# A hybrid-attention encoder layer: the last 448 tokens' attention moved beside the first 640 tokens' feed-forward

## The chip, the cores and the metric

The kernel runs on one core of a Trainium2 chip. The core has a matrix engine (PE, TensorE), two elementwise engines that are used for most of the rest (DVE, VectorE, and POOL, GpSimd), an engine for functions and copies (ACT, ScalarE), and a queue (SP, SyncE) from which this kernel issues its DMA transfers. The metric is device time of one execution in microseconds (us).

## The reference

One layer over 1024 prompt tokens and 64 sample tokens with a past of 128 keys, d_model 1024, in float32. Eight heads use stick-breaking attention (sb: no softmax, a product of keep-probabilities along the keys), eight use forgetting attention (fox: softmax with a cumulative bias).

```python
h = rmsnorm(x, g_mix) * (1.0 + scale) + shift
parts = jnp.split(h @ w_in, SPLITS, axis=-1)          # q, k, v of sb and of fox, forget gates
...
log_keep = jnp.where(mask, jax.nn.log_sigmoid(-z), 0.0)              # sb, z = q k / 8
between = lax.cumsum(log_keep, axis=3, reverse=True) - log_keep
a = jnp.where(mask, jnp.exp(jax.nn.log_sigmoid(z) + between), 0.0)
...
p = jax.nn.softmax(jnp.where(mask, s, -jnp.inf), axis=-1)            # fox, s = q k / 8 + fq - fk
...
o = jnp.concatenate([rmsnorm(o_sb.reshape(b, t, SB_WIDTH), g_sb_out),
                     rmsnorm(o_fx.reshape(b, t, FOX_WIDTH), g_fox_out)], axis=-1)
x = x + (1.0 + ada[2]) * (o @ w_o)
h = rmsnorm(x, g_ffn) * (1.0 + ada[4]) + ada[3]
f = (jax.nn.silu(h @ w_gate) * (h @ w_up)) @ w_down                  # 2816 hidden columns
return x + (1.0 + ada[5]) * f
```

A final rmsnorm follows; k, v and the log forget gates are outputs too.

## The kernel before

The activations stand transposed, features on the partitions and tokens along the columns, in three chunks CH of 384, 384 and 320 tokens. Every dense product splits both sides into a high and a low part (fp32r) and takes three matmuls for each block of 128 rows (dense, L422): high times high, low weight times high, high weight times low. A weight tile (512 KB) is loaded as wraw, copied to its high part on ACT and subtracted to its low part on DVE or POOL (split, L171).

For each of eight pairs of heads (sb for pairs 0 to 3, fox for 4 to 7) the kernel runs attention on the pair (L667) and then project_pair, values and setup for the next one (L472, L529, L561) and some of the 16 ada jobs (L766), which compute the six modulation vectors. Attention takes a head's nine query tiles of 128 tokens in the order QT. A tile computes scores into the PSUM bank ps_z (qs against k2 and kl, the high and low parts of k), then the weights a_t: for sb two sigmoids on ACT, a scan over kp on DVE (L711) and a product on POOL (L715); for fox a maximum on DVE, exp on ACT and a product with the reciprocal sum l on POOL (L738). The weights are turned block by block on PE (pt_a, L747), split into the two halves of aT on ACT and DVE (L753), multiplied with the values vv into ps_av (L756) and written to oT_d in DRAM (av_out). The profile shows a block's transpose as one row of pt_a, so a tile with w keys has w/128 of them.

During the attention of the last pairs the sb outputs are read back from oT_d, squared and summed (o_stats, L820), read again, normed and split (sb_norm L859, sb_split); during the last pair the fox outputs follow (fox_prep). Then come the output projection (out_block, acc_o, evacuated into x1 with the residual at L1014 and L1022), the second norm (norm2, L1061) and the FFN for all tokens: eleven groups of two tiles of 128 hidden columns, each with gate and up products (banks gu), silu, the hidden tile split into dh and dl, and the down product of the group (acc_d, L1217 to L1219), which DVE adds to x1 (L1222):

```python
            for c in range(3):
                t0, n = CH[c]
                for m in range(KT):
                    acc = bank(("t", "t", "acc")[m % 3], "acc_d")
                    for i in range(G):
```

The order of instructions on each engine isn't the order of the code: the program is built in a context that moves instructions by a timeline of its own, within what buffers and banks allow. PSUM has eight banks, given out by tags: acc 1, z 3, t 2, u 1, av 1.

## Time and profile before

| | before |
|---|---|
| median of 3 runs (lowest to highest) | 1682.59 us (1679.03 to 1685.3) |
| profiled execution | 1681.39 us, span 1679.2 us |
| mean granted clock of PE | 0.978 |
| busy over the span | PE 1580.3 us (94%), DVE 947.0, ACT 657.1, POOL 604.9 |
| DMA | 141.61 MB, mean 84 GB/s |

Busy time counts an instruction from start to end; matmuls are pipelined, so one that stands alone is counted with its latency, longer than the distance at which matmuls follow each other in an unbroken row. The program has about 9,700 matmuls. Attention and everything ahead of the FFN end at about 870 us; the FFN fills 870 to 1640.

### The profile page before, as it was taken

The page shows a single profiled execution, that of the slowest core. Times are in us where ns is not written, and L with a number is a line of the kernel's source. Part 1 is how long each engine was busy: PE and PEld are TensorE (multiplying, and loading weights), DVE is VectorE, ACT ScalarE, POOL GpSimd, SP SyncE. Part 2 cuts the span into 40 slices and gives each one's busy share as a digit, 9 for nine tenths or more (in the row PEclk, how much of TensorE's full clock was granted, in tenths as well). Part 3 has the DMA queues.
Part 4 walks back from the last instruction along what each step waited for, and adds up shares of the span by engine and source line. Part 5 has one row for each costly group of instructions (what it writes and reads, how often), then busy time and mean ns, then how long its engine had stood idle before and what let it go on. Part 6 is the DMA issues. An engine that isn't in the chain of part 4 may idle for free.

```text
span 1679.2 us, 26182 instructions
## 1 busy us (share of the span) xinstructions
PE 1580.3 (94%) x9822; PEld 1487.7 (89%) x9822; DVE 947.0 (56%) x1828; ACT 657.1 (39%) x1410; POOL 604.9 (36%) x556
## 2 busy tenths in 40 slices
PE   8898998988899977998999999999999999999998
PEld 4697887867888966987989999999999999999997
DVE  5659767598557565676895334334443344334336
ACT  5466656577445553555454021120211112021127
...
GB/s 309 165 102 93 110 92 100 93 78 32 125 121 121 151 144 63 114 184 100 91 101 63 2 76 39 38 51 26 76 15 62 51 26 71 6 76 50 27 26 107
DMA packets 174750, 141.61 MB, mean 84 GB/s; under 512 B 14336, under 2 KB 167584, under 8 KB 174624
## 3 DMA queue, kind: packets, MB, share of 16 engines
...
## 4 chain that ended last, share of the span: by engine, by line
PE 65%; DVE 4%; POOL 2%; DMA 1%; ACT 1%; issue 1%; SPq 1%; DVEq 0%; POOLq 0%; ACTq 0%
PE gu L428 10%; PE gu L429 10%; PE gu L427 10%; PE acc_d L1219 5%; PE acc_d L1217 5%; PE acc_d L1218 5%; PE acc L427 2%; PE acc L428 2%; PE acc L429 2%; PE ps_av L756 2%; PE pt_a L747 2%; PE acc_o L427 2%; PE acc_o L428 1%; PE acc_o L429 1%; PE ps_z L691 1%
## 5 line engine op out<-in xcount | busy, mean ns | idle before, releaser
L428 PE MATMUL gu<-h,wff_l 128*128 128x384 f32 (+1 forms) x1056 | 345.3, 327 | 0.0
L429 PE MATMUL gu<-h,wff_h 128*128 128x384 f32 (+1 forms) x1056 | 345.1, 327 | 0.0
L427 PE MATMUL gu<-h,wff_h 128*128 128x384 f32 (+1 forms) x1056 | 343.5, 327 | 0.0
L1222 DVE SCALAR_TENSOR_TENSOR x<-acc_d,ada,x 128x384 f32<-128x384 f32 (+1 forms) x352 | 167.0, 498 | 251.2 <-PE acc_d L1219 251.1
L1135 POOL TENSOR_TENSOR sums<-sums,sq 128x384 f32<-128x384 f32 (+1 forms) x17 | 16.8, 990 | 774.7 <-ACT sq L1134 770.8
L427 PE MATMUL acc<-h,whi 128*128 128x384 f32 (+1 forms) x576 | 199.5, 346 | 5.7 <-DVE kraw L500 3.2
L428 PEld LDWEIGHTS gu<-h,wff_l 128*128 128x128 f32 x1056 | 198.2, 188 | 0.0
L429 PEld LDWEIGHTS gu<-h,wff_h 128*128 128x128 f32 x1056 | 198.2, 188 | 0.0
L427 PEld LDWEIGHTS gu<-h,wff_h 128*128 128x128 f32 x1056 | 198.0, 188 | 0.0
L429 PE MATMUL acc<-h,whi 128*128 128x384 f32 (+1 forms) x576 | 193.3, 336 | 3.7 <-DVE h L404 3.7
L428 PE MATMUL acc<-h,wlo 128*128 128x384 f32 (+1 forms) x576 | 193.5, 336 | 0.0
L1217 PE MATMUL acc_d<-dh,wdh 128*128 128x384 f32 (+1 forms) x528 | 173.5, 329 | 0.1
L1219 PE MATMUL acc_d<-dl,wdh 128*128 128x384 f32 (+1 forms) x528 | 172.9, 328 | 0.0
L1218 PE MATMUL acc_d<-dh,wdl 128*128 128x384 f32 (+1 forms) x528 | 172.8, 327 | 0.0
L711 DVE TENSOR_TENSOR_SCAN kp<-kp 128x384 f32<-128x384 f32 (+4 forms) x104 | 140.1, 1354 | 37.5 <-ACT kp L707 35.5
L1184 ACT ACTIVATE sg<-gu 128x384 f32<-128x384 f32 (+1 forms) x66 | 31.3, 474 | 279.2 <-PE gu L429 279.2
L1186 ACT CAST dh<-sg 128x384 fp32r<-128x384 f32 (+1 forms) x66 | 32.5, 493 | 269.6 <-DVE sg L1185 269.6
L747 PE MATMUL pt_a<-ident,a_t 128*128 128x128 f32 x608 | 103.9, 283 | 30.3 <-DVE aT L753 17.0
L441 ACT CAST aT<-pt_a 128x384 fp32r<-128x384 f32 (+3 forms) x208 | 98.9, 481 | 82.0 <-PE pt_a L747 70.7
L753 DVE TENSOR_TENSOR aT<-pt_a,aT 128x384 fp32r<-128x384 f32 (+3 forms) x208 | 110.0, 535 | 36.4 <-ACT aT L441 35.5
L715 POOL TENSOR_TENSOR a_t<-a_t,kp 128x383 f32<-128x383 f32 (+6 forms) x104 | 114.1, 1105 | 31.7 <-DVE kp L711 10.3
L427 PEld LDWEIGHTS acc<-h,whi 128*128 128x128 f32 x576 | 111.4, 193 | 10.9 <-DVE kraw L500 3.6
...
## 6 DMA issues: line engine op xcount, KB each, us to landing
...
oT_d<-ot SPq DMA_DIRECT2D x128, 64.0 KB, 2.1
...
```

The costliest lines, as they stand in the source:

```text
L427: pe.matmul(out=acc, lhsT=wh[:, kt, :], rhs=rh[kt], start=st, stop=False)
L428: pe.matmul(out=acc, lhsT=wl[:, kt, :], rhs=rh[kt], start=False, stop=False)
L429: pe.matmul(out=acc, lhsT=wh[:, kt, :], rhs=rl[kt], start=False, stop=sp_)
L441: act.copy(out=out, in_=in_)
L711: dve.tensor_tensor_scan(out=rev, data0=rev, data1=rev, initial=1.0 if b == w else kp[:, b:b + 1], op0=ALU.mult, op1=ALU.min)
L715: eng[E_AM[qt]].tensor_tensor(out=a_t[:, :wm], in0=a_t[:, :wm], in1=kp[:, a + 1:a + 1 + wm], op=ALU.mult)
L747: pe.transpose(out=pt[:, j * P:(j + 1) * P], in_=at[a][:, j * P:(j + 1) * P], identity=ident)
L753: dve.tensor_tensor(out=tl, in0=pv, in1=f32(th), op=ALU.subtract)
L1217: pe.matmul(out=a_, lhsT=wh[:, m, :], rhs=dh[:, t0:t0 + n], start=(i == 0), stop=False)
L1218: pe.matmul(out=a_, lhsT=wl[:, m, :], rhs=dh[:, t0:t0 + n], start=False, stop=False)
L1219: pe.matmul(out=a_, lhsT=wh[:, m, :], rhs=dl[:, t0:t0 + n], start=False, stop=(i == G - 1))
L1222: dve.scalar_tensor_tensor(out=xc[:, a:b], in0=acc[:, a:b], scalar=ada[:, 5, m, s:s + 1], in1=xc[:, a:b], op0=ALU.mult, op1=ALU.add)
```

## The change

The tokens are cut anew, into chunks of 384, 256 and 448. The first two (640 tokens, query tiles 0 to 4) and the last (tiles 5 to 8) go through the kernel at different times.

- Stage A: the projections of a pair are a generator (pair_units) that stops after each chunk of a product; between the stops the driver issues ada jobs and steps of attention for the five tiles QA of each head of the pair before. A step (steps) issues the weights of tile i + 2, the transposes of tile i, and the product with the values of tile i - 1.
- Each head's operands k2, kl, the last 448 columns of qs, and vv are written to DRAM by setup and values (k2_d, kl_d, qs_d, vv_d; 622, 622, 229 and 655 KB).
- The sb outputs' sum of squares, a pass of its own before (o_stats), is taken in o_prep from the same tiles that are normed; out_block on the first 640 tokens follows, beside the last steps of stage A.
- Stage B: the four tiles QBT of each of the 16 heads, 64 in all, are issued as steps between the second half of the output projection, norm2 and the first nine FFN groups of the first 640 tokens; each head's operands are read back one head ahead (load_ops, load_vv). Each half of a hidden tile (72 of them) is followed by its share of the remaining steps.
- Then o_prep for the last chunk stands beside FFN group 9, its output projection and norm2 ahead of group 10, and a second pass of the FFN follows for the 448 tokens alone, which loads and splits the FFN's weights a second time.
- The tables of engine letters (E_AM and others) go; the choices stand in the code. In the first FFN pass the low parts of the gate and up weights are subtracted on POOL, not DVE.

```diff
-CH = ((0, 384), (384, 384), (768, 320))
+CH = ((0, 384), (384, 256), (640, 448))
+QA = (0, 4, 1, 3, 2)
+QBT = (7, 6, 8, 5)
...
-QT = (6, 7, 0, 1, 4, 5, 2, 3, 8)
...
+    k2_d = [spill.tile([P, KW], F32, name=f"k2_d{h}") for h in range(16)]
+    kl_d = [spill.tile([P, KW], F32, name=f"kl_d{h}") for h in range(16)]
+    qs_d = [spill.tile([P, NB], F32, name=f"qs_d{h}") for h in range(16)]
+    vv_d = [spill.tile([P, 10, P], F32, name=f"vv_d{h}") for h in range(16)]
...
-    bank_bufs = {"acc": 1, "z": 3, "t": 2, "u": 1, "av": 1}
+    bank_bufs = {"acc": 2, "z": 2, "t": 2, "u": 1, "av": 1}
...
-        project(wv, v_evac, ptags[6:9])
-        return qraw, kraw, vraw
+        yield 's0'
+        setup(pr, 0, qraw, kraw)
+        yield from project(wv, v_evac, ptags[6:9])
+        yield 'v'
+        values(pr, vraw)
+        yield 's1'
+        setup(pr, 1, qraw, kraw)
...
+            sync.dma_start(out=vv_d[2 * pr + hb], in_=f32(vv[hb]))
+            vvs[pr, hb] = vv[hb]
...
-            sync.dma_start(out=f32(q2[r]), in_=f32(qs[r]))
-            sync.dma_start(out=f32(kl[o]), in_=nfs_d)
+            sync.dma_start(out=f32(q2[r]), in_=f32(qs[r, 0:CB]))
+            if pr == 4:
+                sync.dma_start(out=f32(kl[o]), in_=nfs_d)
+            dve.tensor_copy(out=q2[o], in_=sel[o, h:h + 1].to_broadcast([HD, CB]))
+        H = 2 * pr + hb
+        sync.dma_start(out=k2_d[H], in_=f32(k2))
+        sync.dma_start(out=kl_d[H], in_=f32(kl))
+        sync.dma_start(out=qs_d[H], in_=f32(qs[:, CB:T]))
+        ops[pr, hb] = (qs, k2, kl, q2, 0)
...
+    def steps(tiles, before=lambda i: None):
+
+        n = len(tiles)
+        for i in range(2):
+            before(i)
+            tiles[i][0]()
+        yield
+        for i in range(n):
+            if i:
+                tiles[i - 1][2]()
+            tiles[i][1]()
+            if i + 2 < n:
+                before(i + 2)
+                tiles[i + 2][0]()
+            yield
+        tiles[n - 1][2]()
+        yield
...
-    def o_stats(c, acc):
-
-        t0, n = CH[c]
-        for i in range(0, 4, 2):
-            both = [
-                t_.rearrange("p a b -> p (a b)")[:, 0:2 * n].rearrange("p (k t) -> p k t", k=2)
-                for t_ in (t_lowraw(), f32(ap1.tile([P, 4, 256], F32R, tag="ada_l", name="sq_l")))]
-            for k in range(2):
-                load_o([t_[:, k] for t_ in both], i + k, t0, n)
-            sq = both[0]
-            pool.tensor_tensor(out=sq, in0=sq, in1=both[1], op=ALU.add)
-            act.activation(sq, sq, AF.Square)
-            if i == 0:
-                pool.tensor_tensor(out=acc, in0=sq[:, 0], in1=sq[:, 1], op=ALU.add)
-            else:
-                for k in range(2):
-                    pool.tensor_tensor(out=acc, in0=acc, in1=sq[:, k], op=ALU.add)
...
         t0, n = CH[c]
+        for k in range(4):
+            load_o([o32[k], los[k % len(los)]], 4 * g + k, t0, n)
+            pool.tensor_tensor(out=o32[k], in0=o32[k], in1=los[k % len(los)], op=ALU.add)
+        squares(o32, acc, sq, n, dve)
+        token_cols([acc], chunk_toks(c), 512, col, tag)
...
-    low_finish = low_job(0)
-    for pr in range(8):
-        if pr < 7:
-            wqk = load_qk(pr + 1)
-        if pr == 7:
-            sb_ready()
-        attention(pr, heads, {HK[0]: fox_first, HK[1]: fox_second} if pr == 7 else {})
-        if pr < 7:
...
+    att = steps([tile_of(pr, hb, qt) for pr in range(8) for hb in range(2) for qt in QA])
+    jobs = (None for job in range(16) for _ in ada_job(job))
+    for pr in range(7):
+        at_ = 1 if pr == 0 else 0
+
+        def to(n):
+            global_n = n - at_
+            take(att, max(0, global_n))
+            return max(at_, n)
+
+        for i, s in enumerate(pair_units(pr + 1)):
+            if i % 2 == 0 or pr % 2 and i == 1:
+                take(jobs)
+            at_ = to({'s0': 6, 'v': 8, 's1': 10}.get(s, min(at_ + 1, 9)))
+            if s == 's0' and pr == FG:
...
+    take(jobs, 100)
+    for c in (0, 1):
+        o_prep_a(0, c)
+    take(att, 3)
     for mp in range(4):
...
+        raw, wh, wl = load_w(wo_src(0, mp), 4, 256)
+        split(raw, wh, wl, act, dve)
+        for c in (0, 1):
+            for m in (2 * mp, 2 * mp + 1):
+                out_block(0, m, c, (wh, wl), "acc")
+            take(att)
+    take(att, 20)
+    R.close()
...
+    def load_ops(H):
+        pr, hb = H // 2, H % 2
+        r = slice(hb * HD, (hb + 1) * HD)
+        o = slice((1 - hb) * HD, (2 - hb) * HD)
+        k2 = bq.tile([P, KW], F32R, tag="k2", name=f"k2b{H}")
+        kl = bq.tile([P, KW], F32R, tag="kl", name=f"klb{H}")
+        qs = bq.tile([P, NB], F32R, tag="qs", name=f"qsb{H}")
+        sync.dma_start(out=f32(qs), in_=qs_d[H])
+        sync.dma_start(out=f32(k2), in_=k2_d[H])
+        sync.dma_start(out=f32(kl), in_=kl_d[H])
...
+    def before(i):
+        n = len(QBT)
+        if i == 0:
+            load_ops(0)
+            load_vv(0)
+        if i % n == 0 and i // n + 1 < 16:
+            load_ops(i // n + 1)
+        if i % n == 2 and i // n + 1 < 16:
+            load_vv(i // n + 1)
+
+    att = steps([tile_of(H // 2, H % 2, qt) for H in range(16) for qt in QBT], before)
...
+    o_prep_a(1, 0)
+    left = go_on(1)
+    o_prep_a(1, 1)
+    L.close()
...
+    def ffn(chunks, gus, ds, lo_eng, held=()):
...
+        nxt = None
+        for g0 in range(0, NFF, 2):
+            w0 = nxt if nxt else load_ff(g0)
+            w1 = load_ff(g0 + 1)
+            hid = []
+            for i, ws in enumerate((w0, w1)):
+                dh = fp.tile([P, CB], F32R, tag="dh", bufs=3, name="dh")
+                dl = fp.tile([P, CB], F32R, tag="dl", bufs=3, name="dl")
+                hid.append((dh, dl))
+                for ci, c in enumerate(chunks):
+                    n = CH[c][1]
...
+                    g_ = bank(tg, "gate")
+                    dense(g_[:, :n], *ws[0], rh, rl, n)
+                    yield 'h'
+                    u_ = bank(tg, "up")
+                    dense(u_[:, :n], *ws[1], rh, rl, n)
+                    sg = fp.tile([P, NB], F32, tag="sg", name="sg")
+                    act.activation(sg[:, :n], g_[:, :n], AF.Silu)
+                    dve.tensor_tensor(out=sg[:, :n], in0=sg[:, :n], in1=u_[:, :n], op=ALU.mult)
+                    act.copy(out=dh[:, t0:t0 + n], in_=sg[:, :n])
+                    dve.tensor_tensor(out=dl[:, t0:t0 + n], in0=sg[:, :n], in1=f32(dh[:, t0:t0 + n]), op=ALU.subtract)
+                    yield 'h'
...
+    left = go_on(3)
+    ws = [wslot(wo_src(1, mp), 4, 256, dve) for mp in range(4)]
+    for c in (0, 1):
+        for m in range(KT):
+            out_block(1, m, c, ws[m // 2], ("acc", "acc", "t")[m % 3] if False else "acc")
+            square(sacc, c, x1[m][c], CH[c][1], pool, "sacc")
+            if m % 2:
+                left = go_on(1)
+        norm2(c, "u")
+    first = ffn((0, 1), ("acc",), ("t", "t", "u"), pool, held=(9,))
+    halves = 9 * 8
+    group = h = 0
+    while group < 9:
+        if next(first) == 'g':
+            group += 1
+            continue
+        h += 1
+        n = left - left * (halves - h) // (halves - h + 1)
+        left = go_on(n)
+    take(att, 70)
+    R.close()
+    attP.close()
+    b3 = ctx.enter_context(tc.tile_pool(name="last", bufs=1, side="right"))
+    for g in range(2):
+        n = NB
+        tmp = [b3.tile([P, n], F32, tag=f"h2b{i}_{g}", name=f"o_tmp{g}_{i}") for i in range(8)]
+        hi = [b3.tile([P, n], F32R, name=f"oh{g}_{k}") for k in range(4)]
+        lo = [b3.tile([P, n], F32R, name=f"ol{g}_{k}") for k in range(4)]
+        col = fp.tile([P, 2, 4], F32, tag="col", name="col_o")
+        o_prep(g, 2, tmp[0:4], tmp[4:6], tmp[6], [tmp[7]], hi, lo, col, "av")
+    while next(first) != 'g':
+        pass
+    for g in range(2):
+        for mp in range(4):
+            w = wslot(wo_src(g, mp), 4, 256, pool)
+            for m in (2 * mp, 2 * mp + 1):
+                out_block(g, m, 2, w, "z")
+                if g:
+                    square(sacc, 2, x1[m][2], NB, pool, "sacc")
+    norm2(2, "av")
+    for s in first:
+        pass
+    for s in ffn((2,), ("acc", "z"), ("t", "t", "u", "av"), dve):
+        pass
```

How the order of instructions changes is shown at three places. First PE in the FFN (names: gu, gate and up are the two products into the hidden tile, acc_d the down product, a name ending in b and a number is a tile that was read back). Before:

```order
L427 MATMUL gu_11169<-h_7_0_0_10849,wff_h 128x384
L428 MATMUL gu_11169<-h_7_0_0_10849,wff_l 128x384
L429 MATMUL gu_11169<-h_7_0_1_10850,wff_h 128x384
L1217 MATMUL acc_d<-dh,wdh 128x384
L1218 MATMUL acc_d<-dh,wdl 128x384
L1219 MATMUL acc_d<-dl,wdh 128x384
L1217 MATMUL acc_d<-dh,wdh 128x384
L1218 MATMUL acc_d<-dh,wdl 128x384
```

Now, near the end of stage B, the same products have a tile's transposes, scores and value products between them:

```order
L1126 MATMUL acc_d<-dh,w_l 128x256
L1127 MATMUL acc_d<-dl,w_h 128x256
L720 MATMUL pt_a<-ident,a_t 128x128 x6
L397 MATMUL gate<-h_0_0_7799,w_h 128x384
L397 MATMUL up<-h_0_0_7799,w_h 128x384
L669 MATMUL ps_z<-k2b_10695,qsb_10697 128x384
L670 MATMUL ps_z<-klb_10696,q2b_10701 128x384
L672 LDWEIGHTS identb
L672 MATMUL ps_z<-mask_fox,identb 128x128
L736 MATMUL ps_av<-aT,vvb_10557 128x256 x3
L720 MATMUL pt_a<-ident,a_t 128x128 x4
L398 MATMUL gate<-h_0_0_7799,w_l 128x384
```

In the FFN PE had only the three kinds of products in its row; now an attention tile's steps stand between two products of the gate.

The second place is PE behind the last product of the last pair of heads (acc, the projection), up to the first row of the output projection. Before, in the stretch in which sqacc (the sum of squares of the sb outputs) is reduced into pc, part of the rows is:

```order
L756 MATMUL ps_av<-aT,vv_1_6583 128x256 x5
L747 MATMUL pt_a<-ident,a_t 128x128 x3
L756 MATMUL ps_av<-aT,vv_1_6583 128x256 x6
L747 MATMUL pt_a<-ident,a_t 128x128 x7
L756 MATMUL ps_av<-aT,vv_1_6583 128x256 x3
L747 MATMUL pt_a<-ident,a_t 128x128 x2
L756 MATMUL ps_av<-aT,vv_1_6583 128x256 x6
L202 MATMUL pc<-ones,sqacc 128x1 x8
L202 MATMUL pc<-ones,sqacc 64x1
L221 MATMUL bc_o<-ident,cols_sb_1146 128x128 x3
L221 MATMUL bc_o<-ident,cols_sb_1148 128x128 x2
L221 MATMUL bc_o<-ident,cols_sb_1148 128x64
```

Now the projections end, and ahead of the output projection acc_o there are 65 rows of attention, in all 30 transposes and 23 matmuls into ps_av, with the reduction of o_low (the squares now) between them; the last of them are:

```order
L672 MATMUL ps_z<-mask_fox,identb 128x128
L736 MATMUL ps_av<-aT,vv_0_6308 128x256 x3
L720 MATMUL pt_a<-ident,a_t 128x128 x4
L182 MATMUL bc_o<-ident,col_o 128x128 x3
L720 MATMUL pt_a<-ident,a_t 128x128 x3
L669 MATMUL ps_z<-k_1_6382,qs_1_6381 128x384
L670 MATMUL ps_z<-klp_959,q_1_6388 128x384
L736 MATMUL ps_av<-aT,vv_0_6308 128x256 x2
L720 MATMUL pt_a<-ident,a_t 128x128
L397 MATMUL acc_o<-h_0_0_6397,whi 128x384
```

Before, the rows without a product lay between pair 6's projections and pair 7's; now they lie behind pair 7's projections, and the first product after them is acc_o.

The third place is DVE. Before, in the FFN, it took the evacuations of acc_d (into x), the hidden tiles' products and the weights' low parts:

```order
L1185 TENSOR_TENSOR sg<-sg,gu_12075 128x384
L1222 SCALAR_TENSOR_TENSOR x_4_2_9933<-acc_d,ada,x_4_2_9933 128x256
L1222 SCALAR_TENSOR_TENSOR x_4_2_9933<-acc_d,ada,x_4_2_9933 128x64
L1187 TENSOR_TENSOR dl<-sg,dh 128x384
L1222 SCALAR_TENSOR_TENSOR x_6_2_10037<-acc_d,ada,x_6_2_10037 128x256
L1222 SCALAR_TENSOR_TENSOR x_6_2_10037<-acc_d,ada,x_6_2_10037 128x64
L1222 SCALAR_TENSOR_TENSOR x_7_2_10054<-acc_d,ada,x_7_2_10054 128x256
L1222 SCALAR_TENSOR_TENSOR x_7_2_10054<-acc_d,ada,x_7_2_10054 128x64
L176 TENSOR_TENSOR wff_l<-wraw,wff_h 128x1024
```

Now, where the first FFN groups lie beside the sb heads' tiles of stage B (kp is the scan, aT the low half of the turned weights, x the evacuations):

```order
L685 SCALAR_TENSOR_TENSOR kp<-kp 128x512
L1110 TENSOR_TENSOR dl<-sg,dh 128x256
L685 SCALAR_TENSOR_TENSOR kp<-kp 128x512
L1130 SCALAR_TENSOR_TENSOR x_1_0_6653<-acc_d,ada,x_1_0_6653 128x384
L726 TENSOR_TENSOR aT<-pt_a,aT 128x4x128
L726 TENSOR_TENSOR aT<-pt_a,aT 128x2x128
L1130 SCALAR_TENSOR_TENSOR x_0_0_6637<-acc_d,ada,x_0_0_6637 128x384
L1130 SCALAR_TENSOR_TENSOR x_2_0_6766<-acc_d,ada,x_2_0_6766 128x384
L1130 SCALAR_TENSOR_TENSOR x_4_0_6901<-acc_d,ada,x_4_0_6901 128x384
L685 SCALAR_TENSOR_TENSOR kp<-kp 128x384
L685 SCALAR_TENSOR_TENSOR kp<-kp 128x512
L1130 SCALAR_TENSOR_TENSOR x_3_0_6782<-acc_d,ada,x_3_0_6782 128x384
```

The evacuations of acc_d that had only products around them now stand behind scans of 384 and 512 columns and behind aT.

## Rows read from the trace of the kernel before

**Rows 1.** Stretches of the whole span: length, each engine, clock, DMA share, GB/s

```profile
0.00:100.00 100.00, 88.23 (x483) 61.08 (x484) 57.30 (x129) 53.54 (x105) 39.60 (x40) 0.98 0.71 225
100.00:450.00 350.00, 315.01 (x2093) 281.61 (x2091) 268.77 (x355) 217.47 (x509) 276.33 (x253) 0.99 0.33 89
450.00:600.00 150.00, 144.09 (x972) 131.69 (x970) 88.34 (x247) 83.74 (x203) 108.19 (x92) 0.99 0.46 124
600.00:650.00 50.00, 29.12 (x131) 22.90 (x131) 27.13 (x79) 21.12 (x53) 36.50 (x39) 0.64 0.51 135
650.00:800.00 150.00, 137.08 (x889) 127.47 (x888) 102.77 (x279) 78.02 (x202) 85.75 (x93) 0.96 0.42 118
800.00:870.00 70.00, 65.38 (x392) 63.75 (x391) 60.67 (x116) 31.76 (x62) 37.82 (x24) 0.98 0.28 87
870.00:1640.00 770.00, 770.00 (x4661) 769.79 (x4660) 317.92 (x567) 142.46 (x223) 3.97 (x4) 1.00 0.15 44
1640.00:1680.00 40.00, 31.40 (x214) 29.37 (x212) 24.08 (x63) 28.98 (x58) 16.72 (x17) 0.94 0.30 112
```

**Rows 2.** Timeline of PE in the FFN: start, duration, engine, line, operation, out<-in

```profile
1009.94 0.34 PE L1219 MATMUL acc_d<-dl,wdh 128*128 128x384 f32 x1
1010.11 0.34 PE L427 MATMUL gu<-h,wff_h 128*128 128x384 f32 x1
```

**Rows 3.** Timeline of PE at the first gate matmul

```profile
871.75 0.31 PE L427 MATMUL gu<-h,wff_h 128*128 128x320 f32 x1
871.90 0.31 PE L428 MATMUL gu<-h,wff_l 128*128 128x320 f32 x1
```

**Rows 4.** Timeline of PE inside attention

```profile
528.05 0.98 PE L756 MATMUL ps_av<-aT,vv 128*128 128x256 f32 x7
...
529.23 0.76 PE L747 MATMUL pt_a<-ident,a_t 128*128 128x128 f32 x5
```

**Rows 5.** Groups of PE in 100 to 450: busy us, mean ns, idle ahead and releasers

```profile
L427 PE MATMUL acc<-h,whi 128*128 128x384 f32 (+1 forms) x292 | 100.9, 346 | 4.1 <-DVE kraw L500 3.2 <-ACT qraw L484 0.6 <-DVE kraw L443 0.2
...
L747 PE MATMUL pt_a<-ident,a_t 128*128 128x128 f32 x304 | 51.2, 280 | 18.8 <-DVE aT L753 16.7 <-POOL a_t L715 2.0
L756 PE MATMUL ps_av<-aT,vv 128*128 128x256 f32 x304 | 50.5, 289 | 0.4 <-DVE aT L753 0.3
```

**Rows 6.** Groups of PE in 450 to 600

```profile
L427 PE MATMUL acc<-h,whi 128*128 128x384 f32 (+1 forms) x152 | 52.5, 345 | 0.9 <-ACT qraw L484 0.4 <-DVE kraw L443 0.4
...
L747 PE MATMUL pt_a<-ident,a_t 128*128 128x128 f32 x129 | 21.4, 276 | 1.2 <-DVE sc L805 1.2
```

**Rows 7.** Groups of PE by shape in 600 to 650

```profile
L756 PE MATMUL ps_av<-aT,vv 128*128 128x256 f32 x39 | 9.0, 355 | 4.4 <-DVE aT L753 2.7 <-DVE ot L663 1.7
L747 PE MATMUL pt_a<-ident,a_t 128*128 128x128 f32 x30 | 7.8, 382 | 7.7 <-POOL a_t L738 7.6
```

**Rows 8.** Timeline of the SP queue in 605 to 640

```profile
623.73 2.46 SPq L139 DMA_DIRECT2D lowraw<-oT_d  x4
```

**Rows 9.** Groups of DVE by shape, whole span

```profile
L1222 DVE SCALAR_TENSOR_TENSOR x<-acc_d,ada,x 128x384 f32<-128x384 f32 x176 | 107.5, 617 | 168.5 <-PE acc_d L1219 168.5
L176 DVE TENSOR_TENSOR wff_l<-wraw,wff_h 128x1024 fp32r<-128x1024 f32 x44 | 54.3, 1235 | 53.1 <-ACT wff_h L173 52.3 <-issue 0.8
L711 DVE TENSOR_TENSOR_SCAN kp<-kp 128x384 f32<-128x384 f32 x40 | 52.2, 1309 | 14.0 <-ACT kp L707 13.0
L711 DVE TENSOR_TENSOR_SCAN kp<-kp 128x512 f32<-128x512 f32 x32 | 50.6, 1589 | 15.3 <-ACT kp L707 14.5
...
L176 DVE TENSOR_TENSOR wlo<-wraw,whi 128x1024 fp32r<-128x1024 f32 x12 | 17.4, 1447 | 2.5 <-ACT whi L173 2.4
...
L711 DVE TENSOR_TENSOR_SCAN kp<-kp 128x192 f32<-128x192 f32 x8 | 9.4, 1171 | 3.3 <-ACT kp L707 3.2
```

**Rows 10.** Groups of POOL by shape, whole span

```profile
L779 POOL TENSOR_TENSOR ada_l<-lowraw,ada_h 128x1024 fp32r<-128x1024 f32 x32 | 79.9, 2496 | 25.2 <-ACT ada_h L778 18.6 <-PE pt_ada L792 4.8 <-issue 1.1
...
L572 POOL TENSOR_TENSOR qs<-qraw,qs 64x1088 fp32r<-64x1088 f32 x16 | 46.0, 2876 | 12.6 <-PE pt_xr L353 5.9 <-DVE qs L443 5.2 <-ACT a_t L708 0.7
```

816 lines of the change are left out of this document (322 added, 494 removed).

## The prediction

> **What bounds the kernel now.** I read the stretches first [rows 1]. From 870 to 1640 us PE is busy 770.00 of 770 us at full clock, DVE 317.92, ACT 142.46, POOL 3.97: the feed-forward (FFN) is bound by PE and nothing waits there. Ahead of it no engine is full: in 100 to 450 us PE has 315 of 350, POOL 276, DVE 269, and in 600 to 650 PE has 29 of 50 at a granted clock of 0.64, the only stretch with a low one. So PE is the bound wherever it gets work in time, and the question is how much of its time before the FFN is not work.
>
> Busy time hides some of that, since a lone matmul is shown with its latency. I therefore price PE's work by pitch, the distance of starts in an unbroken row: 0.17 us for 384 columns [rows 2], 0.15 for 320 [rows 3], (0.98 - 0.28)/6 = 0.117 for 256 and (0.76 - 0.27)/4, about 0.125, for one 128-column transpose [rows 4]; about 0.4545 ns a column. Each group of a stretch, count times pitch, gives its work. 100 to 450: 877 product matmuls 145, 304 transposes 38, 304 matmuls into ps_av 36 [rows 5], the smaller groups 83, together 302; the other 48 us are lost. 450 to 600, the fox pairs: 457 products 75, 129 transposes 16 [rows 6], the rest 50; 141 of 150, lost 9. 600 to 650: 39 into ps_av, 30 transposes [rows 7] and small groups, 16 us; lost 34, with no product matmul in it. In the same way 0 to 100 loses 18, 650 to 800 loses 20, 800 to 871.75 (the first gate matmul [rows 3]) loses 8, the FFN 3, the tail from 1640 on 10. **In all 150 us of the 1681.4 are not PE's work.**
>
> The unit of attention is the transpose, one for each block of 128 by 128 weights, 38 to a head. 100 to 450 loses 48/304 = 0.158 us on each, 450 to 600 loses 9/129 = 0.070. Both have products beside the tiles (0.48 and 0.58 us a transpose). What differs is the scan of the sb heads, 1.31 us for 384 columns and 1.59 for 512 on DVE [rows 9], and the transposes in 100 to 450 wait 16.7 us for aT on DVE, in 450 to 600 none [rows 5, 6]. In 600 to 650 it is 34/30, over 1 us: the same work without products.
>
> **What the change takes, adds and moves.** PE's work stays: FFN 22 x 72 matmuls over 1088 columns, 1,723,392 columns, 783 us, in three pieces or in two passes; the order has 9,686 matmuls for 9,678. As the FFN loses only 3 us where it is, putting it beside attention can give back nothing but parts of the other 147. I go through them.
>
> - *Prologue, 18.* Its order hardly changes, and DMA is busiest there (share 0.71 over the first 100 us [rows 1]). Stays 18.
> - *Stage A,* tiles of the first 640 tokens, 15 transposes a head, 240 in all, beside seven pairs of projections (3 x 24 matmuls over 1088 columns, 35.6 us a pair), so 1.04 us of products a transpose. Half at 0.158 and half at 0.070 is 27. Counting the POOL rows of the order at the profile's durations (31 ada_l of 2.5, 14 qs of 2.88 [rows 10], the rest wlo, a_t, ot and vv), POOL has 315 us there against PE's 357, 88%; in 100 to 450 it was 79% and in 450 to 600 72%. More cover, but a fuller POOL: I take 33; ends 17 (all at 0.070) and 38 (all at 0.158).
> - *From the last k-projection to the end of stage B's sb half.* Here lie the last fox tiles of stage A, the out-blocks of 640 tokens, norm2, the first two FFN groups and the 32 sb tiles of the last 448 tokens. Rows of the order at the profile's durations: DVE 262 us (scans 79, of 512, 384 and 192 columns [rows 9]; aT, evacuations of acc_o and acc_d, norms, split products), PE 279. DVE was never fuller than 0.87 in a stretch with attention or out-blocks (800 to 870), and 0.77 in the one with the scans [rows 1]: 262/0.87 = 301 loses 22, 262/0.77 = 340 loses 61. Between them 42. The order also keeps a run of 30 transposes and 23 matmuls into ps_av without a product (the second place shown with the change), much as 600 to 650 had 30 and 39 [rows 7]: the hole is moved rather than filled. What goes is the second reading of the sb outputs (o_stats: its loads stand one behind another on SP at 0.6 us each [rows 8], and POOL adds them up); what comes is o_prep_a's 16 loads ahead of the first out-block. For these waits 8 more: 50; ends 22 and 75, where the whole hole (34) comes back on the middle.
> - *Stage B, fox half,* 184 transposes beside the FFN of 640 tokens, DVE 161 for PE 250: at 0.070, 13; at 0.158, 29.
> - *Last chunk and second FFN.* The 448 tokens' o_prep lies behind FFN group 9 (144 x 640 columns, 42 us of PE), norm2 and two finals behind group 10: 4. In the second pass a group is 29 us of PE with six splits of 1.24 on DVE [rows 9], 7.4, and six loads: hidden, 3 for the joints. The 66 further weight loads (35 MB) and the spilled k, q and v (34 MB written, 34 read) make 142 MB about 245, 150 GB/s on average; 225 GB/s went at a share of 0.71 in the first 100 us [rows 1]. Priced at nothing: the products cover the weights, and a head's operands are asked for four tiles ahead; without that cover a head's k2 and kl, 1.2 MB, would hold PE 5.5 us at that rate. On SP the 64 spilling writes of stage A stand in one row with the weight loads, at 0.6 us each and behind a setup whose last piece is POOL's 2.9 us qs [rows 10]; the weights behind them are asked for a product of 12 us ahead.
> - *Tail, 10.* A last chunk of 448 tokens has four row tiles for three: 12.
>
> Sum: 18 + 33 + 50 + 13 + 4 + 3 + 12 = 133 lost for 150, so 1681.4 - 17 = 1664.4 for the execution; the median of the runs stands 1.2 above the profiled one: **1666 us**. All low ends give 18 + 17 + 22 + 13 + 4 + 3 + 10 = 87 and 1620; all high ones, with 6 + 5 + 14 for the last three, 18 + 38 + 75 + 29 + 25 = 185 and 1718.
>
> A full POOL also slows DVE. A 1024-column subtraction on DVE takes 1.235 us in the FFN, where POOL has 3.97 of 770 us [rows 1, 9], and 1.447 (wlo x12 [rows 9]) in attention, where POOL is 79% busy: 17% more, already in my prices; a rival below takes it further. The Trainium skill ("SBUF — State Buffer", Who interferes with whom) says that a DVE instruction with two SBUF inputs and a GpSimd instruction that reads SBUF exclude each other for the whole instruction. By that rule the sum would be rival 4's 1691 rather than 1666; the 17% bears out a part of it.
>
> **Rivals.**
> 1. *Slower: evacuations queue behind scans.* In stage B's sb half DVE is at 202 us for PE's 223, and acc_o and acc_d are evacuated by it, which takes its rows in order, so each may stand behind a scan of 1.41 us (the mean of 56). PE fills an acc_d every 1.05 us (six matmuls) and has three banks, two shared with pt_a. In the FFN of before L1222 waited for PE [rows 9], never PE for it. For: DVE at 91%. Against: the down products come in runs with two scans between. From 1666 it decides at (1691 - 1666)/60 = 0.4 us for each of 28 acc_o and 32 acc_d; at 0.9, two thirds of a scan, it costs 54: 1720.
> 2. *Nothing gained.* The hole comes back whole behind the last projection (14 of the 34 are not in the sum), and nothing else is won: 1680. For: the order's run without products; POOL at 88%. Against: o_stats is gone.
> 3. *The fill works.* With two tiles in flight the waits fall to 0.070 a transpose everywhere and DVE runs at 0.87: the low ends, 1620. For: 450 to 600 does it. Against: that stretch has no scans.
> 4. *DVE and POOL hold each other up.* If they can't run together in stage B's sb half, its 115 us of DVE rows with two inputs from SBUF (scans, splits, low parts) and POOL's 133 stand one after the other: 248 for PE's 223, 25 more: 1691. For: the 17%. Against: with POOL busy 79% of the time it is only 17%.
>
> **Chances.** The sum with its own spread, 1648 to 1674: 0.37. Rival 3, 1610 to 1648: 0.16. Rival 2, 1674 to 1691: 0.16. Rival 4, half on either side of 1691: 0.06. Rival 1 and the high ends, beyond 1691: 0.25. A difference of 0.5%, 8.4 us, is about what a measurement of this kernel can tell from none. So faster 0.53, same 0.19, slower 0.28. The range, 1614 to 1718, leaves out 0.06 below and 0.12 above; that of the likeliest case alone is 1648 to 1674.
>
> **What would show it.** In the changed kernel: PE over 93% in stage B's fox half with FFN products beside pt_a; a stretch of low PE right behind the last projections, some 20 to 30 us lost; in the sb half DVE near 90%, PE waiting for aT or x; POOL above 80% in stage A; PE 100% busy in the last 320 us. Wrong would be: PE waiting above all for acc_o and acc_d evacuations (rival 1), for k2b or klb transfers (my zero for DMA), or for a_t on POOL throughout stage A.

## The result: slower, and the profile after

| | before | after |
|---|---|---|
| median (lowest to highest) | 1682.72 us (1679.03 to 1685.3, 4 runs) | 1782.8 us (1778.88 to 1789.11, 4 runs) |
| ratio, 95% interval | | 1.06 [1.0563, 1.0637] |
| mean granted clock of PE | 0.978 | 0.951 |

The change costs 100 us; the prediction was 1666 with 1718 as its upper end. The page of after, engines over the span and then the time slices of PE's clock:

```profile
PE 1627.7 (92%) x9814; PEld 1479.7 (83%) x9814; DVE 995.1 (56%) x1864; ACT 806.2 (45%) x1546; POOL 674.0 (38%) x590
...
PEclk9999987989899689989999999999999989999999
```

PE is busy 47 us longer than before with the same work (priced by pitch, the distance of starts in an unbroken row, as in the prediction: its span less the time lost is 1527 us after, 1529 before). Stretches of after, columns as in [rows 1]:

```profile
0.00:100.00 100.00, 91.22 (x509) 63.35 (x509) 53.77 (x125) 50.59 (x100) 40.50 (x39) 1.00 0.80 258
100.00:200.00 100.00, 97.55 (x644) 90.52 (x644) 62.20 (x79) 52.87 (x126) 61.76 (x59) 0.98 0.51 160
200.00:300.00 100.00, 76.97 (x451) 64.13 (x449) 66.47 (x83) 52.92 (x119) 65.78 (x60) 0.83 0.55 171
...
600.00:700.00 100.00, 82.71 (x477) 73.98 (x476) 71.97 (x155) 53.68 (x119) 48.49 (x54) 0.82 0.49 151
700.00:800.00 100.00, 78.55 (x486) 69.28 (x485) 86.25 (x123) 70.89 (x147) 63.69 (x61) 0.91 0.37 119
...
100.00:600.00 500.00, 436.14 (x2664) 385.01 (x2663) 263.50 (x477) 226.74 (x523) 290.69 (x255) 0.91 0.53 164
...
1420.00:1440.00 20.00, 13.59 (x60) 10.48 (x60) 8.22 (x19) 10.67 (x21) 4.36 (x6) 0.74 0.63 210
```

The reader is to see two holes with a lowered clock, 200 to 600 (stage A) and 600 to 800 (behind the last projections), where before had one [rows 1]. The last line is the joint between the two passes of the FFN. In 100 to 600 no engine is full (POOL 58%, DVE 53%), and PE idles 63.9 us. Its work there is 393 us by pitch, so 107 are lost: each idle microsecond comes with 0.7 more in instructions at the lower clock or with their latency showing.

Lost time (a stretch less PE's work in it by pitch) by the prediction's terms:

| term | predicted | measured in after |
|---|---|---|
| prologue, 0 to 100 | 18 | 15 |
| stage A, 100 to 555 | 33 (17 to 38) | 97 |
| last k-projection to end of stage B's sb half, 555 to 918 | 50 (22 to 75) | 83 |
| fox half of stage B, 918 to 1188 | 13 (13 to 29) | 20 |
| last chunk and joints, 1188 to 1480 | 7 | 21 |
| second FFN's rest and tail, 1480 to 1777 | 12 | 14 |
| sum | 133 | 250 |

What PE waits for in after, whole span (total, times, longest):

```profile
PE ps_z L669 <- ACT a_t L706: 22.6, 15, 5.5
PE ps_z L669 <- ACT a_t L682: 9.2, 6, 4.0
PE pt_v L517 <- ACT vst L519: 9.0, 9, 1.8
PE pa L785 <- POOL ada_l L781: 6.8, 4, 2.9
PE pt_ada L795 <- DVE arow L791: 6.6, 3, 4.3
...
PE ps_z L669 <- DMA k<-k: 4.7, 2, 4.2
PE acc_d L1125 <- DVE x L1130: 4.2, 5, 1.5
```

No wait dominates: score banks held until ACT has read them, and the ada job's own steps (pa, pt_ada). The evacuations of acc_d, rival 1, cost 4.2 us. What SP waits for in 200 to 600 of after:

```profile
SPq L775 <- POOL ada_l L781: 48.1, 13, 9.2
SPq L626 <- DVE lowraw L624: 18.6, 9, 3.5
SPq L603 <- DVE fg L602: 15.7, 1, 15.7
SPq L553 <- POOL qs L541: 15.1, 6, 3.6
```

L775 is the load of an ada job's weights into the one lowraw tile; it waits until POOL has read the last job's. L553 is a spilling write (qs_d) behind POOL's qs. The worst piece of stage A, in a timeline of DVE and POOL:

```profile
232.14 0.74 DVE L685 TENSOR_TENSOR_SCAN kp<-kp 128x256 f32<-128x256 f32 x1
...
246.73 0.72 DVE L410 CAST qs<-qraw 64x1088 fp32r<-64x1088 f32 x1 [3.20 <-ACT qraw L449]
247.58 2.50 POOL L541 TENSOR_TENSOR qs<-qraw,qs 64x1088 fp32r<-64x1088 f32 x1 [1.07 <-PE ps_z L672]
247.84 5.21 DVE L685 TENSOR_TENSOR_SCAN kp<-kp 128x128 f32<-128x128 f32 x2 [0.39 <-ACT kp L681]
250.16 2.35 POOL L137 TENSOR_TENSOR wlo<-wraw,whi 128x1024 fp32r<-128x1024 f32 x1
...
256.49 2.33 POOL L781 TENSOR_TENSOR ada_l<-lowraw,ada_h 128x1024 fp32r<-128x1024 f32 x1
256.57 2.83 DVE L410 CAST qs<-qraw 64x1088 fp32r<-64x1088 f32 x1
...
297.60 0.50 DVE L685 TENSOR_TENSOR_SCAN kp<-kp 128x128 f32<-128x128 f32 x1
```

The row of 5.21 us is two scans merged, of 128 and 256 columns (2.52 and 2.77 us), where such scans take 0.50 and 0.74 with no long POOL row beside them. POOL runs qs and wlo over that time, and the scans end 0.54 us after wlo. The cast takes 0.72 us alone and 2.83 beside ada_l, ending 0.58 behind it. PE at the same place:

```profile
253.41 0.47 PE L795 MATMUL pt_ada<-ident,arow 128*128 128x128 f32 x2 [4.26 <-DVE arow L791]
...
258.88 0.37 PE L785 MATMUL pa<-ada_l,cs 128*4 128x256 f32 x1 [2.92 <-POOL ada_l L781]
259.05 0.41 PE L785 MATMUL pa<-ada_h,cs 128*4 128x256 f32 x1
259.26 0.41 PE L785 MATMUL pa<-ada_l,cs 128*4 128x256 f32 x1
...
264.11 1.12 PE L517 MATMUL pt_v<-ident,vraw 128*128 128x128 f32 x4 [3.58 <-DVE arow L789]
286.43 0.55 PE L669 MATMUL ps_z<-k,qs 128*128 128x256 f32 x1 [4.15 <-DMA k<-k]
```

PE's order has the ada job between tiles and values, so it stands still for an adaptive vector that nobody needs yet. After the idle time its 256-column matmuls follow each other at 0.21 us, not the 0.117 of [rows 4]: the lower of the two clock levels, 1.2 GHz.

### The profile page after: what moved, and what is told of

It is laid out like the page before. It is cut to its first block, busy times and chain, and to the rows that moved or that the text cites. A ratio compares the mean times of both kernels' runs of the same rounds, so it can differ in the third digit from the quotient of the medians.

```text
span 1776.7 us, 26819 instructions
## 1 busy us (share of the span) xinstructions
PE 1627.7 (92%) x9814; PEld 1479.7 (83%) x9814; DVE 995.1 (56%) x1864; ACT 806.2 (45%) x1546; POOL 674.0 (38%) x590
## 5 line engine op out<-in xcount | busy, mean ns | idle before, releaser
L134 ACT CAST w_h<-wraw 128x1024 fp32r<-128x1024 f32 x144 | 149.1, 1049 | 214.2 <-PE acc_d L1127 99.4
L137 POOL TENSOR_TENSOR w_l<-wraw,w_h 128x1024 fp32r<-128x1024 f32 x52 | 125.0, 2411 | 226.7 <-ACT w_h L134 226.7
L397 PE MATMUL acc<-h,whi 128*128 128x384 f32 (+2 forms) x576 | 198.9, 347 | 1.2 <-ACT vraw L456 0.7
L398 PE MATMUL acc<-h,wlo 128*128 128x384 f32 (+2 forms) x576 | 196.7, 342 | 0.0
L399 PE MATMUL acc<-h,whi 128*128 128x384 f32 (+2 forms) x576 | 195.4, 341 | 0.1
L1125 PE MATMUL acc_d<-dh,w_h 128*128 128x384 f32 (+2 forms) x528 | 174.2, 331 | 4.2 <-DVE x L1130 4.2
L1126 PE MATMUL acc_d<-dh,w_l 128*128 128x384 f32 (+2 forms) x528 | 173.1, 328 | 0.0
L1127 PE MATMUL acc_d<-dl,w_h 128*128 128x384 f32 (+2 forms) x528 | 169.5, 328 | 0.0
L685 DVE TENSOR_TENSOR_SCAN kp<-kp 128x384 f32<-128x384 f32 (+3 forms) x104 | 130.4, 1260 | 34.6 <-ACT kp L681 33.0
L397 PE MATMUL gate<-h,w_h 128*128 128x448 f32 (+2 forms) x352 | 122.1, 347 | 3.5 <-ACT w_h L134 1.7
L399 PE MATMUL gate<-h,w_h 128*128 128x448 f32 (+2 forms) x352 | 120.8, 343 | 1.9 <-DVE h L1035 1.9
L397 PE MATMUL up<-h,w_h 128*128 128x448 f32 (+2 forms) x352 | 120.0, 341 | 1.2 <-ACT w_h L134 1.0
L399 PE MATMUL up<-h,w_h 128*128 128x448 f32 (+2 forms) x352 | 119.8, 340 | 0.0
```

The source lines that it names most:

```text
L134: act.copy(out=hi, in_=raw)
L137: lo_eng.tensor_tensor(out=lo, in0=raw, in1=f32(hi), op=ALU.subtract)
L397: pe.matmul(out=acc, lhsT=wh[:, kt, :], rhs=rh[kt], start=st, stop=False)
L398: pe.matmul(out=acc, lhsT=wl[:, kt, :], rhs=rh[kt], start=False, stop=False)
L399: pe.matmul(out=acc, lhsT=wh[:, kt, :], rhs=rl[kt], start=False, stop=sp_)
L685: dve.tensor_tensor_scan(out=rev, data0=rev, data1=rev, initial=1.0 if b == w else kp[:, b:b + 1], op0=ALU.mult, op1=ALU.min)
```

## Theories and experiments

Theory 1: in stage A the ada jobs pace PE. All four steps of a half job (load, ACT's cast, POOL's subtraction, PE's pa) go through one lowraw and one ada_l tile, and in after a half job is asked for at every other stop of the order. Theory 2: DVE and POOL hold each other up (the mechanism of rival 4, but in stage A). Theory 3: the spilling writes on SP, priced at nothing. Theory 4: banks or the short distance of the tiles. Theory 5: the split itself and the hole behind the projections. Each time is one execution's, except where a number of executions is given; the kernel before took 1682 to 1687 us beside them, and executions of one kernel lie up to 10 us apart, so a difference under 10 us is not told from none.

**Banks (a_z3).** Three score banks and one for products, as before had, for two and two. The products' bank tags in the out-blocks and in both FFN passes change with it (not in the lines shown).

```diff
-    bank_bufs = {"acc": 2, "z": 2, "t": 2, "u": 1, "av": 1}
+    bank_bufs = {"acc": 1, "z": 3, "t": 2, "u": 1, "av": 1}
```


> The changed kernel with the banks of before: z 3 and acc 1 instead of z 2 and acc 2; gate takes acc and up takes u, the down product only t. Theory banks (the score products ps_z wait for ACT to read one of only two z banks, 31.8 us of PE's idle time in the changed kernel): these waits fall below 10 us and the time to about 1740. Theories lock, queue and jobs: ps_z waits a little less, time 1770 to 1795, since a single acc bank takes back what a third z bank gives.

Measured: 1818.18, 35 slower. PE's waits for ps_z on ACT fall from 31.8 to 19.2 us, but 100 to 600 loses as much as in after, within 2 us: stage A is not short of score banks. What is added lies behind 600, most of it in 800 to 1500, where the products had lost banks.

**POOL's subtractions on DVE (a_pool2dve; a_ada_dve the last of the three alone).**

```diff
-            pool.tensor_tensor(out=qs[o], in0=qraw[r, :T], in1=f32(qs[r]), op=ALU.subtract)
+            dve.tensor_tensor(out=qs[o], in0=qraw[r, :T], in1=f32(qs[r]), op=ALU.subtract)
-    split(raw, hi, lo, act, pool if c0 >= 1536 or c0 in (0, 512, 1024, 128) else dve)
+    split(raw, hi, lo, act, dve)
-            pool.tensor_tensor(out=lo, in0=raw, in1=f32(hi), op=ALU.subtract)
+            dve.tensor_tensor(out=lo, in0=raw, in1=f32(hi), op=ALU.subtract)
```


> The changed kernel with POOL's long subtractions ahead of the FFN (qs 2.9 us, ada_l 2.4 us, wlo 2.4 us) on DVE. Theory lock (a scan on DVE and a long subtraction on POOL hold each other up, so every link of a tile's chain is stretched): the mean scan of 384 columns falls from over 1.2 us to about 1.0, stage A (100 to 600 us, 105 us lost) loses 60 to 75, time about 1740 although DVE takes about 75 us more rows. Theories banks, queue and jobs: DVE only gets fuller, 1783 or more.

> The changed kernel with ada_l alone on DVE (1.2 us) instead of POOL (2.4 us). Theory period: 32 links of the chain get 1.2 us shorter, so most of the 27 us that all three moved subtractions gave come from this one: 1755 to 1765. Theory lock, where every long POOL row counts alike (32 ada_l, 16 qs, 12 wlo): about half, 1767 to 1773.

Measured: 1755.29, 27 faster, and 1768.68, 14 faster. More work on DVE, and its scans get shorter. Scans by shape in after, and DVE's share of the wlo rows there:

```profile
L685 DVE TENSOR_TENSOR_SCAN kp<-kp 128x384 f32<-128x384 f32 x40 | 50.2, 1256 | 10.8 <-ACT kp L681 9.7
...
L137 DVE TENSOR_TENSOR wlo<-wraw,whi 128x1024 fp32r<-128x1024 f32 x12 | 22.0, 1836 | 16.2 <-ACT whi L134 16.1
...
L685 DVE TENSOR_TENSOR_SCAN kp<-kp 128x256 f32<-128x256 f32 x16 | 19.1, 1193 | 12.7 <-ACT kp L681 12.7
```

and with the three subtractions on DVE, engines over the span first:

```profile
PE 1619.8 (92%) x9814; PEld 1477.6 (84%) x9814; DVE 1008.4 (58%) x1928; ACT 804.9 (46%) x1545; POOL 528.3 (30%) x526
...
L685 DVE TENSOR_TENSOR_SCAN kp<-kp 128x384 f32<-128x384 f32 x40 | 43.0, 1076 | 7.7 <-ACT kp L681 6.6
...
L781 DVE TENSOR_TENSOR ada_l<-lowraw,ada_h 128x1024 fp32r<-128x1024 f32 x32 | 41.9, 1308 | 16.0 <-ACT ada_h L780 16.0
L137 DVE TENSOR_TENSOR wlo<-wraw,whi 128x1024 fp32r<-128x1024 f32 x28 | 38.0, 1359 | 21.3 <-ACT whi L134 16.0 <-DMA out<-vst 5.1
...
L541 DVE TENSOR_TENSOR qs<-qraw,qs 64x1088 fp32r<-64x1088 f32 x16 | 22.8, 1427 | 1.3 <-ACT qs L408 0.8
...
L685 DVE TENSOR_TENSOR_SCAN kp<-kp 128x256 f32<-128x256 f32 x16 | 11.8, 739 | 2.1 <-ACT kp L681 2.1
```

The 256-column scan falls from 1.193 to 0.739 us, its time with no long POOL row beside it. DVE takes over 81 us of rows (41.9, 22.8, and 16.0 more of wlo) and is busy only 13 us more: its other rows shrink by 67. Theory 2 holds. How much of the 27 us is the hold-up is not shown: the moved rows also get shorter, 81 us on DVE for 146 off POOL, and no run parts the two. The Trainium skill ("SBUF — State Buffer", Who interferes with whom) says that a DVE instruction with two SBUF inputs excludes a GpSimd one that reads SBUF, and that a copy or cast can do so too; the two scans and the cast of the timeline (5.21 us, and 2.83 for 0.72) agree.

**The ada jobs left out (a_noada; b_noada in the kernel before).**


> The changed kernel without the 16 ada jobs of stage A (left out: four of the six modulation vectors, which are set to one). PE's own work in them is 34 us. Theory jobs (PE takes the jobs' rows in order and stands behind their load, copy, subtraction and sum): stage A loses 40 to 60 us less besides, time 1690 to 1710. Theories banks, lock and queue: 34 us of work and a small share of waits, 1735 to 1750; with lock toward 1735, since POOL's 77 us of ada_l go as well.

> The kernel before without the 16 ada jobs (left out: four of the six modulation vectors, set to one), beside the changed kernel without them, which took 1677.6, 105 us less than with them for 34 us of PE's work. Theory jobs are worse placed in the changed kernel: before gains only 35 to 50 us, about 1640, so that of the 100 us some 55 to 70 go with the jobs. Theory jobs cost waits in either (they are no part of the loss by the change): before gains 80 or more, below 1605.

Measured: 1677.56, 105 faster, and 1607.96, 76 faster (its before took 1684.04). The jobs' matmuls are 34 us in both; the other 71 and 42 are what they cost beside their work: 29 more in after, what ada_l holds up on DVE included. a_noada is below all its forecasts, and b_noada, forecast at 1640 or below 1605, lies nearer the second: more than half of what the jobs cost, they cost in before too. Without the jobs the change still costs 70 us (1677.56 for 1607.96).

**The ada jobs dealt out (a_spread).** Five half jobs to a pair at fixed stops, for six or seven.

```diff
-            if i % 2 == 0 or pr % 2 and i == 1:
+            if i in (0, 2, 5, 7, 10):
                 take(jobs)
```


> The changed kernel with five half ada jobs for each pair of projections instead of six or seven. Theory period (a half job runs through one buffer: load, copy on ACT, 2.4 us subtraction on POOL, product; one every 8 to 10 us at best, while stage A gives it only the work of two projection stops, some 8.5 us, so the jobs set its pace): 25 to 40 us less, 1745 to 1760, lost time in 200 to 300 us below 20. Rival: each job costs PE its waits wherever it stands, 1778 to 1788.

Measured: 1754.55, 28 faster; SP's wait for ada_l in 200 to 600 falls from 48.1 to 36.0 us, though that wait is no price: without the spills, below, it grows to 59.2 while the time falls. The 256-column scans do not get shorter in it (1.361 us in the mean), so this gain does not come from them. Theory 1 holds in that where the jobs stand costs time, as the 29 of the pair of runs above says. That the period of the single buffers sets the pace is not shown: 200 to 300 still loses about 24 us, where below 20 was expected, and making each ada_l about 1 us shorter (a_ada_dve) gave 14 us, where the period asked for 18 to 28.

**The spills left out (a_spill1).**


> The changed kernel with the spilling writes of the first head alone (left out: the other 15 heads' 60 writes of k2, kl, qs, vv, 32 MB; stage B reads the first head's for all). Theory queue (these writes wait on SP for setup's last piece and hold up the loads and copies behind them): stage A loses 30 to 50 less, about 1745. Theories banks, lock and jobs: 1775 to 1785.

Measured: 1767.85, 15 faster, short of theory queue's 1745 and a little more than executions differ by. It points to a price for the spills that I had put at nothing.

**Distance (a_near).** Stage A's tiles issued one ahead of their turn, not two.

```diff
+    def steps(tiles, before=lambda i: None, ahead=2):
...
+    att = steps([tile_of(pr, hb, qt) for pr in range(8) for hb in range(2) for qt in QA], ahead=1)
```


> The changed kernel with the weights of stage A issued one tile ahead instead of two. Theory distance (stage A is bound by the length of a tile's chain, because too little lies between the steps while no engine is full): one tile less in flight costs 30 or more, over 1810. Theory lock or jobs alone: the chain's length hardly counts, 1775 to 1795.

Measured: 1781.12, no change. The tiles' own chain is not what stage A waits for; with a_z3, theory 4 falls for stage A.

**The split undone (a_one).**

```diff
-QA = (0, 4, 1, 3, 2)
-QBT = (7, 6, 8, 5)
+QA = (6, 7, 0, 1, 4, 5, 2, 3, 8)
+QBT = ()
...
-        sync.dma_start(out=k2_d[H], in_=f32(k2))
-        sync.dma_start(out=kl_d[H], in_=f32(kl))
-        sync.dma_start(out=qs_d[H], in_=f32(qs[:, CB:T]))
```

Not in the lines shown: a stop of the projections is followed by two tiles, and q2 and one other tag get two and three buffers for three and four.


> The changed kernel with the split of attention undone: all nine tiles of a head run in stage A, two for each stop of the projections, nothing is spilled and no attention is left beside the FFN, which stays in two passes. Theory split (cutting attention in two costs by its spills, its second set of loads and the empty stage A): about 1700 to 1730. Theory distance and jobs (the steps are the harm, wherever the tiles are): stage A loses as much or more with twice the tiles, 1780 to 1830.

Measured: 1757.51, 25 faster, between the two theories' times: without the split it still stands 73 us over the kernel before beside it (1684.04).

**Together (a_comb, and a_one_comb, a_comb_spill1 on top of it).** a_comb is a_spread and a_pool2dve in one; the others add a_one's and a_spill1's edits to it.


> The changed kernel with five half jobs a pair and all three subtractions on DVE. If period and lock are two causes they add: 1715 to 1735. If the moved subtractions helped only by the job chain, spreading adds nothing to them: 1750 to 1760. The split design stays above 1682 in either case.

> Split undone (all nine query tiles in stage A, no spilled operands), and with it the two edits that gained most by themselves: five half ada jobs spread over a pair, and the three subtractions of POOL on DVE. What stays of the change is the order of issue one step apart, the out-blocks and feed-forward in two passes. Theory A (the split and what it brings, spills and a hole moved behind the projections, holds what is left of the loss): 1745 - 25 = 1720 at most, and by adding all three gains to 1783 (25, 28, 27) 1703, within 20 us of before. Theory B (the three edits cure the same lost time, and what is left lies in the two passes of the feed-forward and their joints): no better than a_comb, 1740 to 1750, with its loss behind 800 us.

> a_comb without 15 of 16 heads' spilling writes; stage B reads head 0's operands for all heads, so its output is not the reference's. Theory A (SP's row of writes and DMA traffic still cost what they cost before the other two edits): 1745 - 15 = 1730. Theory B (the spills only cost while the ada chain was late, since both wait in the same places): 1740 to 1748. If the hole behind the last projections closes with it (over 30 us), the reload of the operands is what fills that hole.

Measured: a_comb 1744.85, 38 faster than after where its parts sum to 55, between the two theories' times. On top of it the split undone gives 8 more (1736.66; 25 by itself) and the spills 2.4 (1742.42; 15 by itself). These gains are not separate prices: the edits cure in part the same waits, and once the ada chain and the hold-up are gone, spills cost nothing that can be told, and the split's 8 us are not told from none either. Without the spills the hole in 500 to 800 stays as in a_comb, within 2 us.

**The kernel before with the three subtractions on DVE (b_pool2dve, b_p2d_timed the same kernel again; b_ada_dve moves ada_l alone).**

```diff
-E_QL = 'pp'
-E_AJ = 'p'
-LCP = (0, 512, 1024, 128)
-E_LC = 'dp'
+E_QL = 'dd'
+E_AJ = 'd'
+LCP = ()
+E_LC = 'dd'
```


> The kernel before with the same long subtractions (qs, ada_l, wlo of the projections) on DVE instead of POOL. Theory lock: if scan and long POOL rows hold each other up in the kernel before too, it gains as the changed one did (27 us there), 1655 to 1670. Rival: DVE, 269 of 350 us there already, becomes full and the time is 1690 or more.

> The kernel before with qs, ada and wlo subtractions on DVE instead of POOL, timed in rounds: 1652 (one look gave 1652.2), ratio to before 0.98 to 0.985, if the hold-up between DVE and POOL costs before 32 us; if that one look was chance, within 0.5% of before.

> The kernel before with ada_l alone on DVE; with qs and wlo too it took 1652.2, 32 us less. Theory period: the jobs don't set the pace there (a head pair has 18 tiles between them), so ada_l alone gives at most a third, 1670 to 1680. Theory lock, every long POOL row alike: half of it or more, 1662 to 1670.

Measured: 1652.2 for 1684.04 in one execution; 1652.85 for 1684.09 as medians of four and seven, ratio 0.9805 [0.9776, 0.9834]; with ada_l alone 1675.31 for 1686.75, 11 of it. Moving the three rows gains some 31 us in the kernel before too, and this version beats both kernels. Stretches of it:

```profile
100.00:600.00 500.00, 467.02 (x3127) 423.58 (x3126) 387.28 (x683) 309.80 (x737) 279.01 (x309) 0.98 0.39 106
600.00:900.00 300.00, 276.48 (x1713) 262.64 (x1713) 212.29 (x514) 144.56 (x331) 134.18 (x135) 0.95 0.36 105
900.00:1200.00 300.00, 300.00 (x1811) 300.00 (x1811) 119.61 (x211) 47.02 (x73) 0.00 (x0) 1.00 0.15 43
```

of a_one_comb:

```profile
100.00:600.00 500.00, 466.47 (x3109) 419.08 (x3108) 375.26 (x636) 302.90 (x712) 253.11 (x288) 0.98 0.35 95
600.00:900.00 300.00, 236.70 (x1391) 208.39 (x1390) 202.08 (x490) 142.73 (x335) 127.52 (x138) 0.86 0.33 91
```

and of a_comb:

```profile
100.00:500.00 400.00, 369.08 (x2346) 329.46 (x2344) 242.01 (x443) 196.67 (x447) 140.97 (x169) 0.95 0.53 163
500.00:800.00 300.00, 252.75 (x1538) 227.38 (x1536) 208.50 (x392) 160.66 (x351) 139.04 (x147) 0.89 0.49 155
800.00:1200.00 400.00, 382.55 (x2625) 367.93 (x2624) 235.79 (x462) 216.51 (x390) 154.70 (x134) 0.99 0.41 127
1200.00:1500.00 300.00, 290.29 (x1686) 274.25 (x1685) 143.95 (x282) 104.91 (x162) 67.41 (x43) 0.98 0.29 88
```

Lost time by pitch in the three: in 100 to 600 b_p2d_timed 48 and a_one_comb 48, the same; a_comb 54 in its shorter stage A, 100 to 500. In the 300 us behind: 43, 108, and 82. Then b_p2d_timed loses nothing up to its tail, a_one_comb 2 to 1200 and 20 at the last chunk (1200 to 1500), a_comb 28 beside the tiles (800 to 1200) and 20. So a_comb's 92 us over b_p2d_timed are 40 in the hole, 27 beside stage B's fox half, 19 at the last chunk, 6 in stage A, 3 in the tail, less 3 in the prologue: stage A loses little more than b_p2d_timed's 100 to 600, though still more than the 33 predicted, and the rest lies behind the last projections. a_one_comb, which has nothing of the split left, still stands 84 over b_p2d_timed, 65 of it in 600 to 900 (not behind 800, where its theory B had put it): that lies in what it keeps of the change, above all the new order of out-blocks and tiles and the FFN in two passes, not in attention beside the FFN.

**The hole (a_comb_cover, a_one_cover).** The out-blocks of 640 tokens dealt one to a tile step behind the last projections; the lines are a_comb_cover's, and a_one_cover has the same in a_one_comb.

```diff
-    take(att, 3)
+    take(att, 1)
...
                 out_block(0, m, c, (wh, wl), "acc")
-            take(att)
+                take(att)
```


> a_comb with the sixteen out-blocks of the first 640 tokens dealt one to a tile step behind the last projections (1 step ahead of them and 8 pairs of an out-block and a step, for 3 bare steps, 4 with two out-blocks each, and a bare rest); nothing else. Theory A (what is left of the loss is tiles that stand bare, with no product beside them, behind the last projections): of a_comb's 82 us lost in 500 to 800, the 38 of 550 to 625 shrink by half or more: 1745 - 20 = 1725, with the loss of 500 to 800 near 60. Theory B (what is lost there is the waits of the out-blocks themselves, for POOL's sums and DVE's low parts, and DVE at 80 to 90%): 1738 to 1750.

> The same dealing in a_one_comb, where the last pair has 18 tiles and the out-blocks come two to two steps: now one out-block to each step. Theory A: of the 108 us lost in 600 to 900, the 46 of 650 to 750, nearly bare, shrink by half or more: 1737 - 25 = 1712 or less. Theory B: 1730 to 1742; the loss moves but does not shrink, because the out-blocks are then late for norm2 and the feed-forward.

Measured: 1743.21 and 1744.77, against 1744.85 and 1736.66 without: theory A of these runs falls. The loss in 600 to 900 of a_one_cover is 111 (108 without), that of a_comb_cover in 500 to 800 within 2 us of a_comb's 82; only its place moves. What PE waits for in a_one_cover in 550 to 900:

```profile
PE ps_z L665 <- ACT a_t L702: 18.7, 13, 3.8
PE acc_o L397 <- DVE x L885: 7.0, 4, 3.0
PE ps_av L732 <- DVE aT L722: 6.2, 5, 3.7
PE pc L163 <- POOL sacc L1008: 5.7, 1, 5.7
PE pc L163 <- DVE o_low L814: 5.5, 3, 4.8
```

Tiles, out-blocks, their norms and norm2 each wait for a chain of ACT, DVE and POOL, and the 28 us of sb out-blocks that are ready do not fill it however they are dealt. Which chain ends last there is not settled; in the kernel before, 95 us of out-blocks lie in that stretch (all 1088 tokens), in these versions 56, since the last 448 tokens' are held back for the second FFN. That fits, but no run here tried it alone.

## Why the prediction was wrong

- **The step that failed: "Half at 0.158 and half at 0.070 is 27 ... I take 33" for stage A.** It measured 97; these 64 us are more than half of the 117 by which the sum was off. A rate of loss per transpose, read in the kernel before, was carried to an order that issues other work between the tiles. That rate is no property of a tile: a_near moved the tiles' distance for nothing, while a_spread (28) and a_pool2dve (27), 38 together, left the tiles as they are. What the rest of stage A's loss comes from stays open. The prediction did count POOL's load there (88% of PE) but asked only whether POOL is full, not who stands still while a long POOL row runs or which single tile a chain goes through. POOL was 58% busy in the end, not "above 80%": 266 us in 455, where 315 in some 390 were counted.
- **Rival 4's mechanism was right, its place and price were not.** I put the hold-up into stage B's sb half and took the 17% as its measure. Read one by one, the twelve rows of that mean say something else: ten take 1.20 to 1.23 us, as in the FFN, one 1.68, and one, which met POOL's qs, 3.54. From the trace of before:

```profile
214.04 2.54 POOL L572 TENSOR_TENSOR qs<-qraw,qs 64x1088 fp32r<-64x1088 f32 x1 [1.65 <-DVE qs L443]
214.12 3.54 DVE L176 TENSOR_TENSOR wlo<-wraw,whi 128x1024 fp32r<-128x1024 f32 x1 [0.22 <-ACT whi L173]
```

So it is no slowdown of 17% beside a busy POOL, but a stop of about POOL's whole row (2.33 us more for a row of 2.54) where two meet, and the trace of before already held it. Moving the long rows, which takes the hold-up away, gains 27 us in after and 31 in before, where my 150 lost us held it unseen.
- **"From the last k-projection": 83 for 50.** The mechanism, a hole moved rather than filled with DVE near its limit (86% in 700 to 800, said near 90%), was right and its size 8 over the upper end. Spreading the out-blocks does not mend it, nor does undoing the split.
- **"Priced at nothing" for the spills:** 15 in after, 2 in a_comb. SP's row is the likelier path: a write waits for POOL's qs, and the loads stand behind it, while the traffic, 164 GB/s in 100 to 600, is less than the 225 of [rows 1]. a_spill1 takes away both, so this is not shown.
- **Fox half 20 for 13, last chunk and joints 21 for 7, prologue and tail right.** PE over 93% in the fox half came true (93.61 to 97.58 in each 100 us of 800 to 1200). Of the 21, some 11 lie in 1420 to 1440, at the joint of the two FFN passes, where PE is busy 13.59 of 20 us at a clock of 0.74, and 4 in 1340 to 1360, among the last chunk's out-blocks; I had 3 for all joints and 4 for the chunk. PE's work, 1527 for 1529, was as counted.
- **Rival 1 fell** (4.2 us of waits for acc_d's evacuation), and rival 3 needed the fill to work without new waits.
